# Fewer, longer steps for the mixers beside the projections of a hybrid decoder layer

## The chip, the cores and the metric

The kernel runs on one core of a Trainium2 chip. The metric is device time in microseconds (us) of one execution. The engines are named as the profile names them: PE is the matrix engine TensorE (PEld its weight loads), DVE is VectorE, ACT is ScalarE, POOL is GpSimd, SP is SyncE, which here issues the DMAs. A product on PE reads its operands from on-chip memory and writes to one of eight accumulation banks (PSUM), from which ACT or DVE must take the result before the bank can be used again; taking it out is called evacuation.

## The reference

One inference step of a one-layer decoder trunk, for a prompt of 2048 tokens and 8 samples of 8 tokens (64 columns), model width 1024, all in float32:

- h = RMSNorm(x) * (1 + scale) + shift, with scale and shift from a conditioning vector.
- One input projection h @ w_in. Its columns go to two mixers.
  - A gated DeltaNet (4 heads, 128 x 128 state): a causal convolution of width 4 and SiLU on q, k, v; q and k normalised; then chunks of tokens, in each of which a triangular system (A + I) is solved, giving T, and a state S of each head is carried from chunk to chunk: u = T(v b) - T(k b e^G) S, o = (q e^G) S + (q k^T decay) u, S = S c + k_tail^T u. The output is normalised and gated by SiLU(z).
  - Sliding-window attention (8 query heads, 2 key and value heads of 64, window 128) with a relative-position bias and a learned sink in each softmax.
- x = x + gate * (mixers' outputs @ w_out), then RMSNorm, a gated feed-forward block with a causal convolution of width 3 between up- and down-projection, a residual, and a last RMSNorm.

Outputs are the tokens of prompt and samples and the new states and caches.

## The kernel before

Tokens lie along the free dimension, channels along the 128 partitions. The prompt is worked in two halves: the first of two blocks of 512 tokens, the second of blocks of 384, 384 and 320 (the last 64 of these are the samples). Each float32 projection is done as three products of a high and a low part: w_hi*h_hi, w_hi*h_lo and w_lo*h_hi. `gemm_steps` (L360) does these three for one 128-deep slice and then yields; this is one projection step. `project` (L398) runs over weight tiles and blocks and calls an evacuation behind each block.

The mixers are written as Python generators that yield between their stages. They work on chunks of 128 tokens, 8 a half:

- `front` (L675): loads k, q and v of a chunk from DRAM (tiles kq and xv), transposes k and q (kq_ps), takes squares on ACT, computes decays (d_ps, Dc), transposes v (v_ps), makes the matrices A and M (am_ps, tile AM), writes A to DRAM and reads its 16 x 16 diagonal blocks back (G), inverts these in 14 steps of DVE (TU, L764 and L766), writes the inverses to DRAM (tu_d) and reads them back as T and U.
- `levels` (L806): joins the 16 x 16 inverses to 32, 64 and 128 by pairs of products z_ps and u_ps, each with an evacuation between (Y).
- `scan` (L878): p_ps, o_ps, uu_ps, s_ps, o_ps: the chunk's part of the recurrence; `gated_norm` follows, with a transpose ot_ps and a DMA to the tensor mixd.
- `attend` (L970): splits keys and queries into high and low parts on ACT, transposes v (vt_ps), scores for four groups of heads (as_ps), softmax, transposes (pt_ps), masks on POOL (PT), products with v (pv_ps).

`mixers` (L2029) goes over the chunks of a half. For chunk c it runs scan(c), attend(c), levels(c+1) and front(c+2) in `lockstep` (L384): one round takes each generator to its next yield. `ahead` (L2023) does the front of the first two chunks. `beside` (L374) runs rounds of a mixer and, between them, a share of projection steps, which the list SHARE gives: 5.5 steps a round for the first half's mixers, beside the in-projection of the second half, and 4.0 for the second half's, beside the up-projection of the first. What a mixer does not use up is done behind it.

This sets the order in which the program is written. A planner in the framework then orders each engine's instructions: it plays the program through with modelled durations and gives an engine the instruction of the earliest place in the program (its priority) that is ready by that model. On the chip, each engine then takes its instructions in the planned order and waits by semaphore for operands. `tc.issue_after(x)` keeps the block's instructions on x's engine behind x in that order.

The accumulation banks: 2 for the projections ("acc"), 2 for front ("fr"), 2 for attention ("at"), 1 each for scan ("sc") and for levels and gates ("st"). `gates` (L449) computes decays and betas for a half from a small projection (ba_ps), transposed in pieces of 128 tokens (bat_ps) and reduced on DVE.

Of the kernel before, what the change touches and what calls it, by code (L numbers as in the profile page):

```python
# [30 lines left out]
H = 4  # L31
# [63 lines left out]
def kernel(  # L95
# [264 lines left out]
    def gemm_steps(ps, w, hb, n, ks=range(KT), first=None, last=None):  # L360

        (wh, wl), (hh, hl) = w, hb
        for k in ks:
            for i, (a, b) in enumerate(((wh, hh), (wh, hl), (wl, hh))):
                nc.tensor.matmul(ps[:, :n], a[:, k, :], b[:, k, :n],  # L365
                                 start=first is not False and k == ks[0] and i == 0,
                                 stop=last is not False and k == ks[-1] and i == 2)
            yield True
# [6 lines left out]
    def beside(steps, filler, share):  # L375

        due = 0.0
        for _ in steps:
# [70 lines left out]
    def gates(hf, h, wb, pool):  # L449
# [8 lines left out]
        for bi, c0, n, np_ in blocks(hf):  # L458
# [9 lines left out]
            for t in range(0, n, P):  # L468
# [4 lines left out]
                j += 1  # L473
# [201 lines left out]
    def front(c, d, pool, rows=P):  # L675
        c0 = P * c
        smp = rows < P
        two = 1 if smp else 2
        tle = cst[:rows, C_SLE:C_SLE + rows] if smp else cst[:, C_TLE:C_TLE + P]
        tgt = tgtr[:rows, P:] if smp else tgtr[:, :P]  # L680
# [7 lines left out]
        for i in range(2):  # L688
            nc.gpsimd.tensor_tensor(gm[i][:rows], over_h(tle, rows), over_i(ghl[:rows, i, c].bitcast(F32), rows),
                                    ALU.mult)  # L690
        ss = pool.tile([P, H, 2], F32, tag="ss", name="ss")
        kq_ps = []
        for i in range(2):
# [7 lines left out]
            yield True  # L701
# [23 lines left out]
        v_ps = bank("v_ps", "fr")  # L725
        for h in range(H):
            nc.tensor.transpose(v_ps[:rows, P * h:P * h + P], xv[:, h, :], ident)
        vb = pool.tile([P, H, P], F32, tag="vb", name="vb", bufs=two)
        nc.vector.tensor_tensor(vb[:rows], heads(v_ps)[:rows], over_i(nr[:rows, :, 0], P), ALU.mult)
        yield True  # L730

        AM = pool.tile([P, H, 2, rows], F32, tag="AM", name="AM", bufs=1 if smp else 2)
        for s in range(2):
# [7 lines left out]
            yield True  # L741
# [18 lines left out]
        for j in range(1, BS - 1):  # L760
# [6 lines left out]
            if j % 5 == 0:  # L767
                yield True
# [24 lines left out]
        d.update(vb=vb, Kt=Kt, kq=kq, MT=MT, nr=nr)  # L793
# [12 lines left out]
    def levels(d, pool):  # L806
# [58 lines left out]
        yield True  # L865
# [58 lines left out]
    def gated_norm(c, d, o, xz, pool, rows=P):  # L924
# [12 lines left out]
        for _ in range(4):  # L937
            yield True
# [6 lines left out]
        yield True  # L945
# [23 lines left out]

    def attend(c, c1, ac, kt, loaded, pool):  # L970
# [3 lines left out]
        qs, sv, new = loaded.pop()  # L974
        for b in new:
# [1229 lines left out]
```

## Time and profile before

| what | value |
|---|---|
| time, median of 3 runs | 2621.32 us (2616.15 to 2625.87) |
| the profiled execution, its own time | 2624.72 us |
| its span from first to last instruction | 2622.9 us |
| granted clock of TensorE | 0.996 |
| stage with the first half's mixers (about 345 to 750 us) | 405 us, PE busy 395.5 |
| stage with the second half's front and mixers (about 930 to 1378 us) | 448 us, PE busy 445.1 |
| sample mixers and the rest of their up-projection (to about 1530 us) | 152 us, PE busy 150.1 |

Busy time is the time in which at least one instruction of an engine ran. Matmuls are pipelined: two that follow one another overlap in the profile, so the distance between their starts tells more than their lengths. In a row of instructions, "x8" means eight in a row of one kind, and "[0.28 <-DMA T<-tu_d]" that the engine was idle for 0.28 us until that transfer came. One matmul of plain float32 operands shows as two instructions.

### The profile page before, as it was taken

How to read it: one execution, taken by the hardware profiler on the slowest of the kernel's cores; microseconds unless marked ns; L12 is line 12 of the kernel's file. 1: busy time of each engine (PE TensorE's matmuls, PEld its weight loads, DVE VectorE, ACT ScalarE, POOL GpSimd, SP SyncE). 2: the span in 40 equal slices, each digit the busy share in tenths (PEclk: the TensorE clock that was granted, in tenths of full speed). 3: DMA queues.
4: the chain of work that ended last, by engine and by line, in shares of the span. 5: the costliest groups of instructions: out<-in, count | busy, mean ns of one | idle time of the engine just before them, and what ended most of it. 6: DMA issues, size and time to landing. Idle time of an engine off the chain costs nothing.

```text
span 2622.9 us, 45390 instructions
## 1 busy us (share of the span) xinstructions
PE 2553.1 (97%) x16424; PEld 2216.3 (84%) x16424; DVE 1840.1 (70%) x3633; ACT 1288.9 (49%) x3140; POOL 795.7 (30%) x708
## 2 busy tenths in 40 slices
PE   6999999999999999999999999999999999999998
PEld 5677888888888787777877789999999997888998
DVE  6475579896544687788768665886777675687676
ACT  5464365554343455555544353654555554454453
POOL 2064143334232322233121123345565520022022
PEclk9999999999999999999999999999999999999999
DMA  7787554343556353333345266325555447676454
GB/s 274 252 296 270 155 144 120 98 121 83 125 187 204 116 136 90 106 103 90 85 141 203 95 209 222 116 73 166 169 168 180 167 162 273 210 243 201 144 192 135
DMA packets 315820, 427.62 MB, mean 163 GB/s; under 512 B 82211, under 2 KB 206212, under 8 KB 315332
## 3 DMA queue, kind: packets, MB, share of 16 engines
q1 hardware_dynamic: 315596, 424.73, 50.9%
q8 instruction: 129, 2.11, 0.3%
q14 instruction: 95, 0.78, 0.1%
HBM read 305.07 MB, written 120.57 MB: 162 GB/s over the span
## 4 chain that ended last, share of the span: by engine, by line
PE 74%; DVE 10%; DMA 7%; ACT 3%; issue 2%; POOL 2%; SPq 1%; POOLq 0%; DVEq 0%; ACTq 0%
PE up_ps L365 17%; PE dn_ps L1825 16%; PE in_ps L365 12%; PE op_ps L365 5%; PE uq_b L1611 5%; PE uq_c L1611 2%; PE uq_u L1611 2%; PE uq_g L1611 2%; PE pv_ps L1033 1%; DVE ev L573 1%; PE uq_a L1611 1%; DMA mt<-mixd 1%; PE as_ps L996 1%; PE u_ps L811 1%; DVE w_lo L357 1%
## 5 line engine op out<-in xcount | busy, mean ns | idle before, releaser
L365 PE MATMUL in_ps<-hi,w_hi 128*128 128x512 f32 (+2 forms) x880 | 318.1, 364 | 4.7 <-DVE ev L629 2.1
L365 PE MATMUL in_ps<-lo,w_hi 128*128 128x512 f32 (+2 forms) x880 | 314.7, 358 | 1.5 <-DVE lo L297 1.1
L365 PE MATMUL up_ps<-hi,w_hi 128*128 128x512 f32 (+2 forms) x808 | 314.3, 389 | 1.5 <-ACT sg L568 1.5
L365 PE MATMUL up_ps<-lo,w_hi 128*128 128x512 f32 (+2 forms) x808 | 313.5, 388 | 1.9 <-DVE lo L297 1.9
L365 PE MATMUL in_ps<-hi,w_lo 128*128 128x512 f32 (+2 forms) x880 | 314.7, 358 | 0.0
L365 PE MATMUL up_ps<-hi,w_lo 128*128 128x512 f32 (+2 forms) x808 | 311.6, 386 | 0.1
L1825 PE MATMUL dn_ps<-th,wh 128*128 128x512 f32 (+2 forms) x796 | 271.4, 343 | 5.1 <-ACT th L1713 5.1
L1825 PE MATMUL dn_ps<-tl,wh 128*128 128x512 f32 (+2 forms) x796 | 272.6, 343 | 0.0
L1825 PE MATMUL dn_ps<-th,wl 128*128 128x512 f32 (+2 forms) x796 | 271.1, 342 | 0.0
L357 DVE TENSOR_TENSOR w_lo<-w_raw,w_hi 128x1024 fp32r<-128x1024 f32 x115 | 145.2, 1263 | 87.4 <-ACT w_hi L356 82.5
L356 ACT CAST w_hi<-w_raw 128x1024 fp32r<-128x1024 f32 x126 | 132.0, 1048 | 139.6 <-PE op_ps L365 52.5
L365 PEld LDWEIGHTS in_ps<-hi,w_hi 128*128 128x128 f32 x880 | 165.4, 189 | 30.8 <-issue 8.6
L365 PEld LDWEIGHTS in_ps<-lo,w_hi 128*128 128x128 f32 x880 | 166.0, 189 | 21.2 <-issue 3.8
L365 PEld LDWEIGHTS up_ps<-lo,w_hi 128*128 128x128 f32 x808 | 152.3, 188 | 37.4 <-issue 10.7
L365 PEld LDWEIGHTS up_ps<-hi,w_hi 128*128 128x128 f32 x808 | 152.3, 188 | 35.9 <-issue 8.6
L365 PEld LDWEIGHTS in_ps<-hi,w_lo 128*128 128x128 f32 x880 | 165.8, 188 | 17.8 <-issue 3.6
L365 PEld LDWEIGHTS up_ps<-hi,w_lo 128*128 128x128 f32 x808 | 152.1, 188 | 31.5 <-issue 5.3
L1713 ACT CAST wh<-wr 128x512 fp32r<-128x512 f32 x149 | 92.2, 619 | 165.2 <-PE dn_ps L1825 110.0
L1825 PEld LDWEIGHTS dn_ps<-th,wh 128*128 128x128 f32 x796 | 150.9, 190 | 21.1 <-ACT th L1713 5.5
L573 DVE SCALAR_TENSOR_TENSOR ev<-rb,cw,ev 128x512 f32<-128x512 f32 (+2 forms) x180 | 140.3, 785 | 38.6 <-ACT ev L566 36.9
L1825 PEld LDWEIGHTS dn_ps<-tl,wh 128*128 128x128 f32 x796 | 151.0, 190 | 16.1 <-DVE tl L1714 0.4
L1825 PEld LDWEIGHTS dn_ps<-th,wl 128*128 128x128 f32 x796 | 151.1, 190 | 15.4
(565 smaller groups left out, 6514.3 us busy)
## 6 DMA issues: line engine op xcount, KB each, us to landing
w_raw<-in_w_upT_dram SPq DMA_DIRECT2D x50, 512.0 KB
wada<-in_w_ada_dram SPq DMA_DIRECT2D x48, 512.0 KB
w_raw<-in_w_inT_dram SPq DMA_DIRECT2D x44, 512.0 KB
wr<-ws_d SPq DMA_DIRECT2D x88, 256.0 KB
w_raw<-in_w_outT_dram SPq DMA_DIRECT2D x34, 512.0 KB
d<-act_d SPq DMA_DIRECT2D x33, 512.0 KB
wr<-in_w_downT_dram SPq DMA_DIRECT2D x66, 256.0 KB
proj<-ev SPq DMA_DIRECT2D x44, 256.0 KB
```

What stands on the lines that cost most here:

```text
L356: nc.scalar.copy(hi, raw)
L357: (eng or nc.vector).tensor_tensor(lo, raw, hi.bitcast(F32), ALU.subtract)
L365: nc.tensor.matmul(ps[:, :n], a[:, k, :], b[:, k, :n], start=first is not False and k == ks[0] and i == 0, stop=last is not False and k == ...
L573: nc.vector.scalar_tensor_tensor(out, src(j), w[:, j:j + 1], out, ALU.mult, ALU.add)
L811: mm = lambda out, a, b, r, c: nc.tensor.matmul(out, a, b, start=True, stop=True, tile_position=(r, c))
L996: nc.tensor.matmul(banks[v][:, 256 * g:256 * g + 256 - P * k0], qs[:, 2 * (g0 + g) + v], t[:, v, :2 - k0].rearrange("p w j -> p (w j)"), s ...
L1033: nc.tensor.matmul(pv_ps[64 * v:64 * v + 64, :], (vprev[0], vt)[half][:, 64 * v:64 * v + 64], PT[v, half], start=half == k0, stop=half == 1)
L1611: nc.tensor.matmul(bk[t][:, :nb], u[:, k], v[:, k], start=new and k == 0 and y == 0, stop=k == KG - 1 and y == 2, skip_group_check=True)
L1713: nc.scalar.copy(h, raw)
L1825: nc.tensor.matmul(acc[m, s][:, :n], w[q, i][a][:, c], th[b][:, v], start=new and i == 0 and y == 0, stop=i == KH - 1 and y == 2, skip_gro ...
```

## The change

Five edits. (1) Yields are taken out and moved, so that a chunk's generators have 6 yields or fewer: 7 rounds a chunk instead of 11. `front` does both transposes and squares in one round and both am_ps in one; the transpose of v moves behind the fifth step of the inversion; `attend` transposes v behind the scores, masks both halves in one round, and splits the next chunk's keys and queries at its own end (`attend_split`). (2) The loads of `front` become `front_load`, called for chunk c+3 in chunk c, behind four rounds. (3) SHARE rises to 8.0, 8.4 and 6.1; the sample stage keeps 4.0 by an entry of its own. (4) With `behind`, a round's instructions on PE are ordered behind the last product of `gemm_steps` that was written before it, and everything in the round gets a priority 60 places earlier. This holds for both halves' mixers and the second half's `ahead`. (5) `gates` transposes all pieces of a block into one bank and reduces them together.

```diff
@@ gemm_steps
-                nc.tensor.matmul(ps[:, :n], a[:, k, :], b[:, k, :n],
+                mm = nc.tensor.matmul(ps[:, :n], a[:, k, :], b[:, k, :n],
...
+            product[:] = [mm.ins]
             yield True
+    product = []
-    def beside(steps, filler, share):
+    def beside(steps, filler, share, behind=False):
         due = 0.0
-        for _ in steps:
+        while True:
+            with (tc.issue_after(product[0]) if behind and product else nullcontext()), (tc.high_priority(OFFSET) if behind else nullcontext()):
+                if not next(steps, None):
+                    break
             due += share
@@ gates
-                nc.tensor.transpose(ps[:rows, t:t + 32], ev[:32, t:t + rows], cst[:32, C_ID:C_ID + 32])
-                nc.vector.tensor_reduce(ba[:rows, j, :], ps[:rows, t:t + 32].rearrange("p (a r) -> p r a", r=16)[:, 0:8],
-                                        mybir.AxisListType.X, ALU.add)
+                nc.tensor.transpose(ps[:rows, 32 * i:32 * i + 32], ev[:32, t:t + rows], cst[:32, C_ID:C_ID + 32])
+            for i, m, rows in ((0, n // P, P), (n // P, 1, n % P)):
+                if rows:
+                    v = ps[:rows, 32 * i:32 * i + 32 * m].rearrange("p (j a r) -> p j r a", a=2, r=16)[:, :, 0:8]
+                    nc.vector.tensor_reduce(ba[:rows, j:j + m, :], v, mybir.AxisListType.X, ALU.add)
+                    j += m
@@ front
-    def front(c, d, pool, rows=P):
+    def front_load(c, d, pool, rows=P):
...
+        d.update(kq=kq, xv=xv, gm=gm)
+        yield True
+
+    def front(c, d, pool, rows=P):
...
+        kq, xv, gm = d["kq"], d["xv"], d["gm"]
...
                 nc.scalar.activation(jk[:rows], ps[:rows, h, :], AF.Square, accum_out=ss[:rows, h, i:i + 1])
-            yield True
...
-        v_ps = bank("v_ps", "fr")
-        for h in range(H):
-            nc.tensor.transpose(v_ps[:rows, P * h:P * h + P], xv[:, h, :], ident)
-        vb = pool.tile([P, H, P], F32, tag="vb", name="vb", bufs=two)
-        nc.vector.tensor_tensor(vb[:rows], heads(v_ps)[:rows], over_i(nr[:rows, :, 0], P), ALU.mult)
-        yield True
...
                                                ALU.mult)
-            yield True
...
-            if j % 5 == 0:
+            if j == 5:
+                yield True
+                v_ps = bank("v_ps", "fr")
+                for h in range(H):
+                    nc.tensor.transpose(v_ps[:rows, P * h:P * h + P], xv[:, h, :], ident)
+                vb = pool.tile([P, H, P], F32, tag="vb", name="vb", bufs=two)
+                nc.vector.tensor_tensor(vb[:rows], heads(v_ps)[:rows], over_i(nr[:rows, :, 0], P), ALU.mult)
+            elif j == 10:
                 yield True
...
                 nc.sync.dma_start(dst, TU[nb * h:nb * h + nb, x])
+        yield True
@@ levels
         nc.vector.tensor_copy(U[low, :, high], ut[low, 0])
-        yield True
@@ gated_norm
-        for _ in range(4):
-            yield True
+        yield True
+        yield True
...
-        yield True
@@ attend
+    def attend_split(kt, loaded):
+        qs, _, new = loaded[0]
+        for b in new:
+            for t in kt:
+                nc.scalar.copy(t[:, :, b % 2], t[:, :, b % 2].bitcast(F32))
+        nc.scalar.copy(qs, qs.bitcast(F32))
...
-        qs, sv, new = loaded.pop()
-        for b in new:
-            for t in kt:
-                nc.scalar.copy(t[:, :, b % 2], t[:, :, b % 2].bitcast(F32))
-        nc.scalar.copy(qs, qs.bitcast(F32))
-        vt_ps = bank("vt_ps", "at")
-        nc.tensor.transpose(vt_ps[:, :P], sv, ident)
...
-        yield True
+        qs, sv, _ = loaded.pop()
...
             yield True
+        vt_ps = bank("vt_ps", "at")
+        nc.tensor.transpose(vt_ps[:, :P], sv, ident)
...
                 nc.gpsimd.tensor_tensor(PT[v, half], pt, tri[half], ALU.mult)
-            yield True
+        yield True
+        if loaded:
+            attend_split(kt, loaded)
+        yield True
         pv_ps = bank("pv_ps", "at")
...
-        yield True
         vprev[0] = vt
@@ the plan
-    SHARE = (5.4, 5.5, 4.0, 2.05, (2.0, 1.4), 5.0, (1.3, 2.0), 8.0)
+    SHARE = (8.0, 8.4, 6.1, 2.05, (2.0, 1.4), 5.0, (1.3, 2.0), 8.0, 4.0)
+    OFFSET = 60
@@ ahead
-            yield from front(c0, ds[c0], pool)
-            yield from lockstep(levels(ds[c0], pool), front(c0 + 1, ds[c0 + 1], pool))
+            yield from front_load(c0, ds[c0], pool)
+            yield from lockstep(front(c0, ds[c0], pool), load_next(c0 + 1, pool))
+            yield from lockstep(levels(ds[c0], pool), front(c0 + 1, ds[c0 + 1], pool), load_next(c0 + 2, pool))
+
+        def load_next(c, pool):
+            for _ in range(4):
+                yield True
+            yield from front_load(c, chunks[c], pool)
@@ mixers
+            attend_split(kt, loaded)
...
+                if c + 3 < c1:
+                    g.append(load_next(c + 3, pool))
@@ the calls
-            beside(mixers(0, mp), filler, SHARE[1])
+            beside(mixers(0, mp), filler, SHARE[1], True)
...
-            beside(ahead(1, mp), filler, SHARE[2])
-            beside(mixers(1, mp), filler, SHARE[2])
+            beside(ahead(1, mp), filler, SHARE[2], True)
+            beside(mixers(1, mp), filler, SHARE[2], True)
...
-            beside(lockstep(sample_delta(sp), sample_attend(sp), weight_sums(range(6, KH), sp, nc.vector)), filler, SHARE[2])
+            beside(lockstep(sample_delta(sp), sample_attend(sp), weight_sums(range(6, KH), sp, nc.vector)), filler, SHARE[8])
```

More of the change, by code (lines that the diff above doesn't have):

```diff
@@ L6 @@
-from contextlib import ExitStack
+from contextlib import ExitStack, nullcontext
 import numpy as np
@@ L364, in gemm_steps @@
             for i, (a, b) in enumerate(((wh, hh), (wh, hl), (wl, hh))):
-                nc.tensor.matmul(ps[:, :n], a[:, k, :], b[:, k, :n],
-                                 start=first is not False and k == ks[0] and i == 0,
-                                 stop=last is not False and k == ks[-1] and i == 2)
+                mm = nc.tensor.matmul(ps[:, :n], a[:, k, :], b[:, k, :n],
+                                      start=first is not False and k == ks[0] and i == 0,
+                                      stop=last is not False and k == ks[-1] and i == 2)
+            product[:] = [mm.ins]
             yield True
@@ L467, in gates @@
             ps = st_bank("bat_ps")
-            for t in range(0, n, P):
+            for i, t in enumerate(range(0, n, P)):
                 rows = min(P, n - t)
-                nc.tensor.transpose(ps[:rows, t:t + 32], ev[:32, t:t + rows], cst[:32, C_ID:C_ID + 32])
-                nc.vector.tensor_reduce(ba[:rows, j, :], ps[:rows, t:t + 32].rearrange("p (a r) -> p r a", r=16)[:, 0:8],
-                                        mybir.AxisListType.X, ALU.add)
-                j += 1
+                nc.tensor.transpose(ps[:rows, 32 * i:32 * i + 32], ev[:32, t:t + rows], cst[:32, C_ID:C_ID + 32])
[4 more added lines that the diff above has]
+                    j += m
             yield True
@@ L670, in attn_consts @@
         return NB, own, sink, nsink
-    def front(c, d, pool, rows=P):
+    def front_load(c, d, pool, rows=P):
         c0 = P * c
         smp = rows < P
-        two = 1 if smp else 2
         tle = cst[:rows, C_SLE:C_SLE + rows] if smp else cst[:, C_TLE:C_TLE + P]
-        tgt = tgtr[:rows, P:] if smp else tgtr[:, :P]
         kq = pool.tile([P, H, 2, rows], F32, tag="kq", name="kq", bufs=1 if smp else 3)
@@ L690, in front @@
                                     ALU.mult)
+        d.update(kq=kq, xv=xv, gm=gm)
+        yield True
+    def front(c, d, pool, rows=P):
+        smp = rows < P
+        two = 1 if smp else 2
+        tle = cst[:rows, C_SLE:C_SLE + rows] if smp else cst[:, C_TLE:C_TLE + P]
+        tgt = tgtr[:rows, P:] if smp else tgtr[:, :P]
+        kq, xv, gm = d["kq"], d["xv"], d["gm"]
         ss = pool.tile([P, H, 2], F32, tag="ss", name="ss")
@@ L1011, in attend @@
             yield True
+        vt_ps = bank("vt_ps", "at")
+        nc.tensor.transpose(vt_ps[:, :P], sv, ident)
+        vt = keep.tile([P, P], F32, tag="vt", name="vt", bufs=2)
+        nc.scalar.copy(vt, vt_ps[:, :P])
+        if c == NCH - 1:
+            nc.sync.dma_start(O["p_swa_v"], vt)
         if c + 1 < c1:
@@ L1054, in sample_delta @@
         nc.sync.dma_start(S0, I["state_ssm"].rearrange("p (b h) d -> p b h d", b=NB_S))
+        yield from front_load(NCH, d, sp, LS)
         yield from front(NCH, d, sp, LS)
```

6 lines of the change are left out of this document (1 added, 5 removed).

## The prediction

> **What bounds the kernel now.** I read the page first, then busy time by stage, then the waits of TensorE in the two mixer stages, then TensorE's timeline over one chunk of each.
>
> ```profile
> span 2622.9 us, 45390 instructions
> ...
> PE 2553.1 (97%) x16424; PEld 2216.3 (84%) x16424; DVE 1840.1 (70%) x3633; ACT 1288.9 (49%) x3140; POOL 795.7 (30%) x708
> ...
> PEclk9999999999999999999999999999999999999999
> ```
>
> TensorE (PE) is the bound, at full clock. Busy time by stage says the same of the stages that the change touches (columns: stretch, length, busy time of PE, PEld, DVE, ACT, POOL, then clock and DMA):
>
> ```profile
> 345.00:750.00 405.00, 395.48 (x3243) 350.97 (x3243) 305.73 (x892) 210.59 (x702) 137.56 (x131) 1.00 0.41 111
> 930.00:1378.00 448.00, 445.14 (x3199) 349.40 (x3198) 356.59 (x924) 229.88 (x709) 110.13 (x96) 1.00 0.38 104
> 1378.00:1530.00 152.00, 150.05 (x741) 111.48 (x740) 106.58 (x197) 62.61 (x158) 21.51 (x11) 1.00 0.45 156
> ```
>
> 345 to 750 holds the first half's mixers beside in-projection, 930 to 1378 the second half's beside up-projection. PE is busy for 98% and 99% of them, VectorE (DVE) for 75% and 80%, ScalarE (ACT) for about half. So a gain cannot come from idle time of PE as the page counts it; it has to be time in which PE is "busy" and moves no columns. The timeline shows that time where the products of a mixer stand between two projection products (start us, length, engine, line, tiles):
>
> ```profile
> 507.48 0.34 PE L365 MATMUL in_ps<-hi,w_lo 128*128 128x384 f32 x1
> 507.75 0.68 PE L811 MATMUL z_ps<-T,AM 64*64 64x64 f32 x8
> 508.35 0.45 PE L365 MATMUL in_ps<-hi,w_hi 128*128 128x384 f32 x1
> 508.64 0.34 PE L365 MATMUL in_ps<-lo,w_hi 128*128 128x384 f32 x1
> 508.81 0.33 PE L365 MATMUL in_ps<-hi,w_lo 128*128 128x384 f32 x1
> ...
> 523.91 0.33 PE L365 MATMUL in_ps<-hi,w_lo 128*128 128x384 f32 x1
> 524.09 0.62 PE L716 MATMUL d_ps<-gm,tgtr 128*128 128x512 f32 x2
> 524.54 0.34 PE L365 MATMUL in_ps<-hi,w_hi 128*128 128x384 f32 x1
> 524.72 0.34 PE L365 MATMUL in_ps<-lo,w_hi 128*128 128x384 f32 x1
> ...
> 528.67 0.34 PE L365 MATMUL in_ps<-hi,w_lo 128*128 128x384 f32 x1
> 528.85 0.60 PE L727 MATMUL v_ps<-cst,xv 128*128 128x128 f32 x4
> 529.21 0.42 PE L365 MATMUL in_ps<-hi,w_hi 128*128 128x384 f32 x1
> 529.47 0.34 PE L365 MATMUL in_ps<-lo,w_hi 128*128 128x384 f32 x1
> ```
>
> Two projection products start 0.17 us apart (508.64, 508.81). At z_ps the one before lasts 0.27 to the next start (0.10 over) and the one behind 0.29 (0.12 over): this interruption costs **0.22 us** beside its own work. At v_ps it is 0.01 + 0.09 = **0.10 us**, at d_ps 0.01 + 0.01 = **0.02 us**. The mean of the three is 0.11 us; I call it the edge.
>
> How many such groups a chunk has, I counted on the same view, a group being all mixer products between two projection products: from the p_ps product of one chunk to that of the next there are 19 in the first half, and over the 53 us that follow 1091 there are 16 in the second. The first and the last of each:
>
> ```profile
> 500.25 1.05 PE L884 MATMUL p_ps<-S,kq 128*128 128x128 f32 x8
> ...
> 556.39 0.34 PE L811 MATMUL u_ps<-inv,Y 32*32 32x32 f32 x10 [0.20 <-ACT Y L841]
> ...
> 558.93 1.05 PE L884 MATMUL p_ps<-S,kq 128*128 128x128 f32 x8
> ...
> 1091.23 0.67 PE L811 MATMUL u_ps<-inv,Y 64*64 64x64 f32 x8
> ...
> 1138.81 1.93 PE L1033 MATMUL pv_ps<-PT,vt 128*64 128x512 f32 x6
> ```
>
> The second thing PE loses is waits for operands. The longest of each mixer stage (engine, line, waited for: us in total, times, longest):
>
> ```profile
> PE u_ps L811 <- DVE Y L859: 2.7, 1, 2.7
> PE pv_ps L1033 <- POOL PT L1028: 1.8, 3, 1.0
> PE u_ps L811 <- ACT Y L841: 1.5, 3, 0.7
> ...
> PE p_ps L884 <- DVE xz L942: 1.2, 2, 0.8
> PE z_ps L811 <- DMA T<-tu_d: 1.0, 3, 0.5
> PE u_ps L811 <- DVE Y L859: 0.5, 1, 0.5
> ```
>
> These six make 8.7 us in 13 waits, 0.67 us each. They are small because ready projection products nearly always cover a mixer's latency.
>
> **The change part by part.** *Steps.* A chunk's longest generator falls from 11 rounds to 7, and the share of projection steps per round rises from 5.5 to 8.4 (first half) and from 4.0 to 6.1 (second): 60.5 against 58.8 and 44 against 42.7 a chunk. So projection work beside a chunk stays the same and no mixer product is added or removed; only its place changes. A round grows from 405 / 8 / 11 = 4.6 us to 405 / 8 / 7 = 7.2 us. If all products of a round stand together, a chunk has 7 groups. Some will not: a round's second product can be late (v_ps now follows DVE work within its chain, vt_ps follows the last scores), and the gates keep their own ba_ps and bat_ps places. I allow 2 strays, 9 groups. Removed: (19 - 9) x 8 + (16 - 9) x 8 = 136 groups, x 0.11 = **15 us**. Bounds: 7 groups and 0.22 us each give (12 + 9) x 8 x 0.22 = 37 us; at the 0.02 us of d_ps, or if the strays are as many as now, nothing.
>
> *Behind and 60 places up.* The order edge holds a round's products behind the preceding round's last projection product, which takes away early strays; the priority makes the same products, and all of the mixers' DVE, ACT, POOL and queue work, go ahead of the projection work that comes within 60 places. This is the edit that can add waits. ACT in the first half, by shape:
>
> ```profile
> L700 ACT ACTIVATE junk<-kq_ps 128x128 bf16<-128x128 f32 x48 | 13.3, 277 | 1.2 <-PE kq_ps L697 0.3
> L590 ACT ACTIVATE rb<-ev 128x384 f32<-128x384 f32 x24 | 12.6, 527 | 26.7 <-DVE ev L573 26.7
> ...
> L563 ACT COPY rb<-in_ps 128x384 f32<-128x384 f32 x24 | 11.3, 472 | 3.6 <-PE in_ps L365 3.4
> ...
> L700 ACT ACTIVATION_READ_ACCUMULATOR junk<-kq_ps 128x1 f32 x48 | 9.5, 199 | 0.0
> ```
>
> The front's first round now has both squarings: 8 x (277 + 199) ns = 3.8 us on ACT in one piece, where it had 1.9 us twice. Behind it stand the projection's evacuations (L563, 0.47 us, and its companion). An accumulation bank has 24 products x 0.17 = 4.1 us until PE wants it back, plus the mixer products in between; 3.8 us fits under that, so I cost it at nothing; without that cover it is the rest of 3.8 us once a chunk. The d_ps product, one round later, wants one of the two banks that the squarings read: 7.2 us later, against 3.8 us of ACT work.
>
> *Waits.* Longer rounds put 7.2 us instead of 4.6 between a product and the one that needs its evacuation. That serves the level products (2.7, 1.5, 0.5), pv_ps (now two rounds behind PT) and z_ps behind T (1.0); p_ps behind xz is not helped. I take 6 of the 8.7 us, bounds 0 and 8.7. For new waits I put 3 of 0.67 us, **+2 us**, bounds 0 and half of the 2 x 8 x 7 = 112 rounds, 37 us.
>
> *Loads ahead.* front_load issues three DMAs on SP and two products on POOL one chunk earlier:
>
> ```profile
> L689 POOL TENSOR_TENSOR gm<-cst,ghl 128x512 fp32r<-128x512 f32 x10 | 12.0, 1203 | 5.4 <-PE d_ps L716 4.5 <-DVE AM L738 1.0
> ```
>
> and SP's own waits in the same stage:
>
> ```profile
> SPq L635 <- DVE ev L591: 39.6, 11, 10.2
> ```
>
> The same number of both; POOL is busy for 34% of the stage and its 2 x 1.2 us lie beside other work. On SP they pass stores of the projection that hold the queue (L635, 39.6 us over 11 waits); a load comes in the fifth of seven rounds, three rounds or some 20 us ahead of its front, and a store delayed by three issues holds an ev buffer, not PE. Cost 0. The keys' split on ACT moves from the head of a chunk to its sixth round, work unchanged. In the second half the attention's bias loads share the kq buffers, all three of which are now taken when mixers start; they wait for the first chunk's o_ps, two rounds, with projection products as cover: 0 on PE.
>
> *Gates.* The transposes of a block now fill one bank one behind the other, and 4 reductions replace 9 in the second half's gates (2 replace 8 in the first); their groups are in the 19. *Sample.* Its share stays 4.0 on fewer rounds, so more up-projection is left behind it, all of it PE work in any order: 0.
>
> Sum: -15 - 6 + 2 = **-19 us**. The profiled execution took 2624.72 us (span 2622.9 and 1.8 around it), so 2605.7; the median shown is 3.4 us under that execution, so **2602 us** against 2621.32.
>
> **The rivals.** *Edges are free (2615 us).* If most groups are like d_ps, grouping is worth nothing and only the 6 us of waits go. For it: d_ps at 0.02 us. Against: z_ps at 0.22 and v_ps at 0.10, both seen. [...]
>
> *The planner places them as before (2621 us).* The order edge binds a round's products only to what lies before; nothing holds the next projection products behind them. If operands come late in the plan, groups stay scattered. For it: a product that late data splits today, with another mixer product put in between,
>
> ```profile
> 1106.37 0.23 PE L811 MATMUL z_ps<-T,AM 32*32 32x16 f32 x2 [0.28 <-DMA T<-tu_d]
> ...
> 1106.98 0.71 PE L871 MATMUL uu_ps<-vb,inv 128*128 128x128 f32 x4
> 1107.62 0.23 PE L811 MATMUL z_ps<-T,AM 32*32 32x16 f32 x2
> ```
>
> Against: rounds of 7.2 us, in which such data has more time to come.
>
> *Everything merges at the dear price (2578 us).* 37 us of edges and 6 of waits off. For it: the price at z_ps, and six such level products a chunk. Against: v_ps and d_ps.
>
> *Waits multiply (2644 us, slower).* Grouped products are issued in order on PE; one whose operand is late holds its whole group and the projection behind it, where it now stands alone at a place where it was ready. Place: d_ps behind the squarings, u_ps behind Y. With the 0.67 us of a wait, 31 of the 112 rounds eat the 21 us of gain; at every second round it is 56 x 0.67 - 15 = 23 us slower. For it: ACT stands 26.7 us in all behind one kind of instruction (L590), which waits for DVE, so late evacuations do queue. Against: PE waited 13 times for long in 16 chunks, and rounds get longer. [...]
>
> **How the numbers follow.** About 0.5%, 13 us, can be told from no change. Forecast (2592 to 2611): 0.47, of which 0.41 is faster by more than that and 0.06 within. Everything merges: 0.15, faster. Edges free: 0.16, and placed as before: 0.10, both within. Waits multiply: 0.12, slower. Faster 0.56, same 0.32, slower 0.12. The range 2580 to 2632 holds all but the lower part of the merging case and the larger part of the last one.
>
> **What would show it.** Right: about 9 groups a chunk in PE's timeline; chunks of about 56.5 and 51 us instead of 58.7 and 53; the six waits down to some 3 us; the stages behind 1530 us unmoved. Wrong: chunks of the old length with half the groups (edges were free), or rows of PE waiting on DVE or ACT that sum to 20 us and more (waits multiply), or 15 and more groups a chunk (not placed).

## The result and the profile after

The changed kernel takes 2643.99 us (median of six runs, 2638.55 to 2647.82). The kernel before, run beside it, takes 2625.93 us (median of six, 2616.15 to 2628.45). The ratio is **1.0072, 95% interval 1.0059 to 1.0085**: 18 us slower. The forecast was 2602 us, 19 us faster than the 2621 it started from and 24 us faster than the kernel before in these runs; its range ended at 2632. The profiled execution of the changed kernel took 2638.55 us, and 2624.72 us is that of before.

Where the time came from shows first in when the stages begin. Three marks, each the first product of its kind in TensorE's timeline: the output projection of the first half starts at 779.5 us before and 781.5 after (2 us later); the first quarter of the last up-projection at 1730.9 and 1745.1 (14.2 later); the down-projection at 2152.7 and 2166.2 (13.5 later). So the stage with the first half's mixers gave and took the same, and the one with the second half's lost some 12 us. Page and busy time by stage of the changed kernel, the same two stretches as before:

```profile
span 2636.8 us, 45371 instructions
...
PE 2556.4 (97%) x16424; PEld 2223.9 (84%) x16424; DVE 1837.0 (70%) x3622; ACT 1287.6 (49%) x3141; POOL 798.0 (30%) x708
...
345.00:750.00 405.00, 393.14 (x3259) 354.34 (x3258) 315.61 (x891) 210.13 (x704) 140.74 (x132) 1.00 0.41 113
930.00:1378.00 448.00, 440.28 (x3134) 344.85 (x3133) 344.89 (x911) 223.16 (x691) 102.09 (x88) 0.99 0.36 96
```

In the first stretch PE starts 3259 products where it started 3243; in the second 3134 where it started 3199, with 5 us more idle time and a clock of 0.99. Its waits there (engine, line, waited for: us in total, times, longest), first half from 345 to 760 us, then second half from 900 to 1410 us:

```profile
PE ot_ps L958 <- POOL o L953: 2.4, 2, 1.3
PE z_ps L829 <- ACT cout L578: 1.9, 2, 1.4
PE in_ps L365 <- ACT sb L588: 1.7, 2, 1.2
PE in_ps L365 <- ACT ev L575: 1.5, 1, 1.5
...
PE ot_ps L958 <- POOL o L953: 1.7, 1, 1.7
PE z_ps L829 <- DVE T L869: 1.6, 2, 1.3
PE o_ps L908 <- DVE vb L903: 1.2, 2, 0.8
```

None of these seven was among the six quoted of before; two kinds of them, z_ps behind T and o_ps behind vb, did stand in the first half of before, with 1.1 us each. The old ones did shrink (pv_ps behind PT is gone, u_ps behind Y fell from 4.7 us in all to 2.1), and others took their place: ot_ps, now two rounds behind the scaling of o instead of four, and projection products behind evacuations on ACT.

And the products stand otherwise than the change was to place them. TensorE's timeline of the changed kernel, second half (start us, length, engine, line, tiles; the pair behind the names is the size of the piece of the array that the product uses):

```profile
1114.98 0.60 PE L888 MATMUL uu_ps<-vb,inv 128*128 128x128 f32 x4
1115.52 0.23 PE L829 MATMUL z_ps<-T,AM 32*32 32x16 f32 x2
1115.67 0.49 PE L888 MATMUL uu_ps<-vb,inv 128*128 128x128 f32 x2
1116.09 0.23 PE L829 MATMUL z_ps<-T,AM 32*32 32x16 f32 x2
1116.25 0.49 PE L888 MATMUL uu_ps<-vb,inv 128*128 128x128 f32 x2
...
1121.12 0.49 PE L916 MATMUL s_ps<-u,Kt 128*128 128x128 f32 x2
1121.54 0.21 PE L829 MATMUL u_ps<-inv,Y 32*16 32x16 f32 x2
1121.68 0.49 PE L916 MATMUL s_ps<-u,Kt 128*128 128x128 f32 x2
1122.10 0.21 PE L829 MATMUL u_ps<-inv,Y 32*16 32x16 f32 x2
1122.24 0.49 PE L916 MATMUL s_ps<-u,Kt 128*128 128x128 f32 x2
```

The rows above the dots lie within one "group" by the prediction's count, the rows below within another: no projection product stands between the rows of either. Inside, two kinds alternate two by two. From one pair of s_ps to the next is 0.56 us; where products of these forms follow their like, the median distance of starts is 0.11 us for s_ps and 0.007 for u_ps, so two and two would take 0.24. One turn there and back costs 0.32 us.

**An account of TensorE.** To put the three losses side by side I took, for each product, the time from its start to the next start, less the median distance of that kind to its like in the kernel before. What is left went to one of three: half-clock stretches (the granted clock in the record is 0.5); a wait, where the record has an operand arriving more than 0.12 us after the product could have started; and the rest, called changes, which is mostly what changing from one kind to another costs. First half: from 247.8 us to the first output-projection product; second half: from the first up-projection product to the first of the quarters.

| kernel | first half: length, changes, waits, half clock | second half: length, changes, waits, half clock |
|---|---|---|
| before | 531.7, 33.9, 15.9, 1.5 | 859.2, 47.5, 14.9, 1.4 |
| after | 533.7, 29.7, 20.3, 3.1 | 871.5, 53.5, 17.4, 4.7 |
| e1 few steps alone | 535.4, 29.3, 20.0, 4.5 | 861.1, 37.4, 20.1, 8.1 |
| e2 second half plain | 531.9, 29.5, 19.8, 1.5 | 859.2, 38.4, 19.2, 6.1 |
| e6 old steps, edge and priority | 545.3, 40.4, 19.3, 2.9 | 860.2, 43.7, 18.1, 3.4 |
| e7 eight rounds | 532.9, 29.7, 18.6, 3.1 | 862.4, 50.8, 12.5, 3.3 |
| e10 lead 30 | 536.5, 29.5, 20.2, 6.0 | 854.0, 45.5, 8.9, 4.2 |
| e12 lead 30, second half plain | 533.1, 30.0, 20.6, 1.5 | 842.1, 35.0, 10.2, 1.5 |
| e13 before with lead 30 | 534.5, 33.5, 16.3, 3.6 | 855.9, 47.7, 9.2, 3.2 |

The products' own time is the same within 3 us in every row (480 to 483 and 795 to 796). One profiled execution differs from the next of the same kernel: in e8, whose first part is the kernel before, the first half took 541.0 us, not 531.7. 4.3 us of that lie ahead of the mixers: 247.8 us is the start in every row, and the first kq_ps product runs at 247.8 us before, 247.9 after, 251.4 in e6 and 252.1 in e8. So the account says which kind of loss moved; how much a kernel gains or loses is said by the timed runs.

Against before, the changed kernel has 4.2 us less of changes in the first half, which 4.4 us of waits and 1.6 us of half clock eat up; and 6.0 us more of changes, 2.5 us more of waits and 3.3 us more of half clock in the second. The line between changes and waits is not sharp: where every idle gap over 0.12 us counts as a wait, whatever ended it, the second half has 4.2 us more of changes and 4.9 us more of waits.

### The profile page after: what moved, and what is told of

Read it like the earlier page. It is cut to its first block, busy times and chain, and to the rows that moved or that the text cites. A ratio compares the mean times of both kernels' runs of the same rounds, so it can differ in the third digit from the quotient of the medians.

```text
span 2636.8 us, 45371 instructions
## 1 busy us (share of the span) xinstructions
PE 2556.4 (97%) x16424; PEld 2223.9 (84%) x16424; DVE 1837.0 (70%) x3622; ACT 1287.6 (49%) x3141; POOL 798.0 (30%) x708
## 3 DMA queue, kind: packets, MB, share of 16 engines
q1 hardware_dynamic: 315596, 424.73, 50.7%
## 4 chain that ended last, share of the span: by engine, by line
PE 57%; DVE 7%; DMA 5%; issue 2%; POOL 2%; ACT 2%; SPq 1%; POOLq 0%; DVEq 0%; ACTq 0%
PE up_ps L365 17%; PE dn_ps L1846 16%; PE op_ps L365 6%; PE uq_b L1632 4%; PE in_ps L365 2%; PE uq_c L1632 2%; PE uq_u L1632 2%; PE uq_g L1632 2%; DMA rawu<-in_w_upT_dram 1%; PE uq_a L1632 1%; DVE TU L776 1%; DVE gt L774 1%; DMA rawg<-in_w_upT_dram 1%; PE pv_ps L1054 1%; DVE w_lo L357 1%
## 5 line engine op out<-in xcount | busy, mean ns | idle before, releaser
L365 PEld LDWEIGHTS in_ps<-lo,w_hi 128*128 128x128 f32 x880 | 166.4, 189 | 19.2 <-DVE lo L297 2.5
L1846 PEld LDWEIGHTS dn_ps<-tl,wh 128*128 128x128 f32 x796 | 151.0, 190 | 16.3 <-DVE tl L1735 0.7
```

The lines of the kernel that those rows point to most:

```text
L365: mm = nc.tensor.matmul(ps[:, :n], a[:, k, :], b[:, k, :n], start=first is not False and k == ks[0] and i == 0, stop=last is not False and ...
L1846: nc.tensor.matmul(acc[m, s][:, :n], w[q, i][a][:, c], th[b][:, v], start=new and i == 0 and y == 0, stop=i == KH - 1 and y == 2, skip_gro ...
```

## Experiments

The kernel before ran beside each; all timed ones in five rounds. Two theories stood at the start. A: the 60 places of priority cost, most in the second half. B: the longer steps cost (squarings in one piece, ot_ps two rounds after its scaling).

**e1: the steps alone.** Neither order edge nor priority anywhere.

```diff
-            beside(mixers(0, mp), filler, SHARE[1], True)
+            beside(mixers(0, mp), filler, SHARE[1])
...
-            beside(ahead(1, mp), filler, SHARE[2], True)
-            beside(mixers(1, mp), filler, SHARE[2], True)
+            beside(ahead(1, mp), filler, SHARE[2])
+            beside(mixers(1, mp), filler, SHARE[2])
```

> The steps as changed (fewer and longer, loads a chunk ahead, gates in one bank), but neither the order edge nor the 60 places, in either half. Theory A, the 60 places cost, most in the second half, where they put products among the projection that are not ready: without them both halves lose that, so 2644 less the 14.6 us of the second half and some of the first half's, 2615 to 2630 us, with PE's waits in 900 to 1410 us back near the 4 us of the kernel before. Theory B, the longer steps cost (both squarings in one piece, the output transposed two rounds after its scaling instead of four): 2638 to 2646 us, the waits on o and on ACT's evacuations stay.

2627.26 us, ratio to before 1.0003 (0.9992 to 1.0013). The loss is gone, as A said; but the waits of the second half did not go back to 4 us as A expected. They grew, on the transfer of T above all:

```profile
PE z_ps L829 <- DMA T<-tu_d: 3.6, 7, 1.8
PE uu_ps L888 <- DVE o L910: 1.8, 1, 1.8
PE z_ps L829 <- DVE T L869: 1.6, 1, 1.6
```

So the fewer, longer steps by themselves do save changes (10 us in the second half by the account) and give all of it back to waits (5 us) and half clock (7 us).

**e2: edge and priority in the first half alone.** The second pair of lines of e1's diff.

> The changed kernel with the order edge and the 60 places in the first half alone. Theory A: the second half's stretch returns to within 5 us of the kernel before, 2626 to 2633 us. Theory B: nothing of the second half's 14.6 us comes back, 2640 to 2646 us.

2623.92 us, 0.9998 (0.9988 to 1.0009): all of the 18 us comes back with the second half alone, a little more than theory A expected. Theory A holds, B falls. The stretch of the changed kernel's timeline shown above has its counterpart here:

```profile
1101.88 1.05 PE L888 MATMUL uu_ps<-vb,inv 128*128 128x128 f32 x8
1103.19 0.60 PE L829 MATMUL z_ps<-T,AM 32*32 32x16 f32 x6
...
1108.53 0.38 PE L829 MATMUL u_ps<-inv,Y 32*16 32x16 f32 x32
1108.74 0.47 PE L829 MATMUL u_ps<-Y,inv 32*32 32x16 f32 x24
1109.14 0.94 PE L916 MATMUL s_ps<-u,Kt 128*128 128x128 f32 x6
```

uu_ps stands whole, and u_ps runs through 56 in a row between two pieces of s_ps. Over the second half s_ps and u_ps change places 2 + 1 times here and 24 + 22 times in the changed kernel, uu_ps and z_ps once against 27 times, z_ps and projection 29 against 48 times.

**e3: the order edge without the priority.**

```diff
-            with (tc.issue_after(product[0]) if behind and product else nullcontext()), (tc.high_priority(OFFSET) if behind else nullcontext()):
+            with (tc.issue_after(product[0]) if behind and product else nullcontext()):
```

> The changed kernel with the order edge and without the 60 places. If it is the 60 places that cost (theory A): as the kernel with neither, within 4 us, 2615 to 2630 us. If the order edge costs, by holding products that are ready behind a projection product: 2640 us and more.

2629.7 us, 1.0010 (0.9996 to 1.0023): within 0.3% of both e1 and before. The edge is not what costs.

**e4: the priority without the order edge.** The other half of that line is kept.

> The changed kernel with the 60 places and without the order edge. In the planned order of TensorE this makes 334 groups of mixer products in the first half and 196 in the second, against 91 and 124 with the edge, 315 more, the products being the same. If a group costs the 0.11 us of the prediction: 35 us more, 2679 us. If edges are free (0.02 us): 2650 us. At the 0.22 us of z_ps: 2713 us.

2674.93 us, 1.0183 (1.0165 to 1.0202): near the middle expectation, but not for its reason alone. By the account the first half has 24 us more of changes than the changed kernel (389 groups in the timeline against 115, 0.09 us for each one more) and another 24 us of half clock. The timeline shows both. Mixer products stand one pair at a time between projection products:

```profile
368.86 0.44 PE L365 MATMUL in_ps<-hi,w_hi 128*128 128x384 f32 x1
369.24 0.21 PE L829 MATMUL u_ps<-inv,Y 32*16 32x16 f32 x2
369.38 0.44 PE L365 MATMUL in_ps<-lo,w_hi 128*128 128x384 f32 x1
...
374.64 0.69 PE L365 MATMUL in_ps<-hi,w_hi 128*128 128x384 f32 x1
375.26 0.29 PE L829 MATMUL u_ps<-Y,inv 32*32 32x16 f32 x2
375.47 0.69 PE L365 MATMUL in_ps<-lo,w_hi 128*128 128x384 f32 x1
```

A projection product and two u_ps take 0.52 us (368.86 to 369.38), where projection products alone start 0.17 apart: again 0.33 us for one turn there and back. Then the clock falls, and the same takes 0.83 us. Busy time in stretches of 3.4 us around that moment (stretch, length, PE, PEld, DVE, ACT, POOL, clock):

```profile
367.96:371.38 3.42, 3.42 (x21) 1.92 (x21) 2.69 (x11) 2.54 (x6) 2.68 (x2) 1.00 0.23 64
371.38:374.80 3.42, 3.42 (x15) 1.92 (x13) 3.13 (x10) 3.42 (x16) 2.10 (x2) 0.50 0.27 81
374.80:378.20 3.40, 3.40 (x13) 1.93 (x13) 3.40 (x9) 2.53 (x10) 2.60 (x3) 0.50 0.00 0
```

PE counts as busy without a break, and its clock is halved all the same, for 17 us.

**e5: a lead of 60 steps.** In the changed kernel the second half's first kq_ps product runs at 919.3 us, 45.7 us behind the first up-projection product (873.6), though its place in the program is the very front: before, it is 918.8, 47.1 behind. By then 57 projection steps have run that were written beside later rounds. The row of the changed kernel:

```profile
919.32 0.93 PE L715 MATMUL kq_ps<-cst,kq 128*128 128x128 f32 x7
```

The kernel of this run lets 60 of them run first by the program too:

```diff
             inverse_tiles(mp)
+            for _ in range(60):
+                next(filler)
             beside(ahead(1, mp), filler, SHARE[2], True)
```

> The changed kernel, with 60 projection steps (some 35 us of up-projection) run off ahead of the second half's first mixer work. In the changed kernel that work's first products run 45 us behind the place where the program has them, because the memory of their tiles comes free late. Theory C, the 60 places cost in the second half because its mixers lag their place in the program, so that the priority pulls products that are never ready together: with the lag gone the second half groups as the first does, and the time is that of the kernel with the 60 places in the first half alone or better, 2612 to 2628 us. Theory D, the 60 places cost wherever the projection beside the mixers is the up-projection: 2638 to 2646 us.

2624.34 us, 0.9994 (0.9985 to 1.0004). Theory C holds as to the loss: with the lead the priority costs nothing against e2. The hoped-for gain did not come: in this profile the output projection behind waits 8.3 us for split weights (op_ps behind DVE w_lo, 2.7 us in e2). The 60 steps are missing there as cover: with the same lead these waits are 9.3 us in e9, with 30 steps 3.4 us in e10 and 1.8 us in e12.

**e6: order edge and priority on the old steps.** The kernel before with the lines of `beside` and the two calls changed.

> The kernel before, steps, loads and gates unchanged, with the order edge and the 60 places added in both halves. If the 60 places cost by themselves in the second half: 2635 to 2645 us. If they cost only with the longer steps, whose groups are larger: within 5 us of the kernel before, 2621 to 2631 us.

2638.02 us, 1.0042 (1.0026 to 1.0059): they cost 11 us by themselves. In this profile the loss lies in the first half, not the second, so the expectation named the right sum and the wrong place. The second half's mixers lag there as in the changed kernel (48.7 us), and the stage took 1 us more than before: what was lost in the changed kernel's second half takes the other edits as well as the priority.

**e7: eight rounds a chunk.** e2 with one more yield before ot_ps, one more at the head of `levels`, shares of 7.35 and 5.34.

> The kernel with the order edge and the 60 places in the first half alone, with eight rounds a chunk instead of seven: one more round between the scaling of o and its transposes, one more between the loads of T and the first z_ps product; shares 7.35 and 5.34. If the gain of the fewer groups is eaten by waits, and by the half-clock stretches that follow them: waits of PE on POOL o and on the DMA of T go from some 8 us over both halves to under 3 us, half-clock stretches become fewer, and the time is 2610 to 2619 us. If the waits go and the time stays at 2622 to 2628 us, the waits were not what ate it.

2627.79 us, 1.0009 (1.0000 to 1.0019). The waits on o are gone, that on T's transfer is down to 1.1 us; in the second half all waits went from 19.2 to 12.5 us and half clock from 6.1 to 3.3. The time did not follow, because changes rose from 38.4 to 50.8 us: with another round the products stand in 167 groups up to the second output projection, where the kernel before has 159 and e2 142. Waits and changes are traded for each other here.

**e8: the two prices by themselves.** The kernel before, with products on constants added behind its end; what they compute is thrown away. Left out below: behind each 48 products a transpose, one to four copies of its result on VectorE, and a transpose that reads the last copy.

```diff
+        for rep in range(16):
+            stream("s_together", 24)
+            for kind in ("bz", "bv", "bd"):
+                small(kind)
+        for rep in range(16):
+            for kind in ("bz", "bv", "bd"):
+                stream("s_apart", 8)
+                small(kind)
+        for width in (128, 640, 1152, 1664):
+            for rep in range(16):
+                stream(f"s_gap{width}", 48)
...
```

> The kernel before with a series of products added behind its end, on constants, in fixed order on TensorE (its results are not stored). First 16 times 24 projection-like products (128x384) and then 8 products of 64x64, 4 transposes and 2 products of 128x512 as one group; then 16 times the same products as three groups, each behind 8 of the 24. The difference of the two, per two groups added, is the price of a group beside its own work: 0.2 us a repetition by the prediction's 0.11 us, 0.04 us if edges are free. Then four series of 16 times 48 products and one wait of TensorE for a chain on VectorE, of one to four instructions (an estimate from VectorE's rows: some 0.6, 1.2, 1.8 and 2.4 us). If a short wait costs half-clock stretches besides itself, the granted clock falls below 1 in the series with the longer waits and not in those with the shorter ones, and a repetition is up to 1.7 us longer than its products and its wait; if only long idle time does that, the clock stays at 1 in all four.

This is one profiled execution. Together, a repetition takes 6.30 us, apart 6.38: **0.04 us for each group more**, not 0.11. The timeline says why. First the three kinds in one group, then each alone:

```profile
2662.04 1.14 PE L2138 MATMUL bz<-sm 64*64 64x64 f32 x16
2663.11 0.66 PE L2142 MATMUL bv<-cst,sm 128*128 128x128 f32 x4
2663.52 0.71 PE L2145 MATMUL bd<-mv,wt 128*128 128x512 f32 x2
...
2760.45 1.14 PE L2138 MATMUL bz<-sm 64*64 64x64 f32 x16
2761.52 1.66 PE L2132 MATMUL s_apart<-mv,wt 128*128 128x384 f32 x8
2763.03 0.60 PE L2142 MATMUL bv<-cst,sm 128*128 128x128 f32 x4
2763.38 1.66 PE L2132 MATMUL s_apart<-mv,wt 128*128 128x384 f32 x8
```

bz takes 1.07 us to the next start in both, whether a transpose or a projection-like product follows. What costs is going between the 128*128 array and a 64*64 piece of it, and both series do that once a repetition. Where bz stands alone, the stream's last product ahead of it takes 0.27 us to the next start instead of 0.17, the first bz 0.11 instead of 0.06, the last 0.15 instead of 0.06, and the stream's first product behind it 0.28 instead of 0.17: 0.34 us for one turn there and back, near the 0.32 of s_ps and u_ps. Between the 128*128 kinds almost nothing is lost: the last transpose of bv takes 0.08 us less to the next start than the others, and the stream's product behind it 0.09 us more.

The second part, waits of rising length. The rows of the wait in the third and fourth series, and busy time and clock over each of the four series:

```profile
3299.87 0.30 PE L2166 MATMUL gb<-cst,g 128*128 128x128 f32 x1 [1.67 <-DVE g L2162]
...
3310.90 0.30 PE L2166 MATMUL gb<-cst,g 128*128 128x128 f32 x1 [2.27 <-DVE g L2162]
```

```profile
2829.00:2975.00 146.00, 140.25 (x801) 135.67 (x799) 4.37 (x15) 0.00 (x0) 0.00 (x0) 1.00 0.00 1
2976.00:3133.00 157.00, 139.84 (x800) 135.51 (x799) 14.22 (x32) 0.00 (x0) 0.00 (x0) 1.00 0.00 1
3134.00:3299.00 165.00, 139.14 (x795) 134.74 (x794) 23.07 (x47) 0.00 (x0) 0.00 (x0) 1.00 0.00 1
3300.00:3484.00 184.00, 149.44 (x800) 145.07 (x799) 31.77 (x61) 0.00 (x0) 0.00 (x0) 0.94 0.00 1
```

Waits of 1.67 us leave the clock at 1; waits of 2.27 us bring six half-clock stretches of 3.41 us in sixteen repetitions, and a repetition with one takes 12.6 us instead of 11.03. So a wait of 2.27 us can cost 1.6 us on top of itself.

**e9 to e14: what the longer steps are worth where the mixers stand at their place.**

e9 is e5 with the second half plain.

> The changed kernel with the 60 steps of up-projection run off first, and the order edge and the 60 places in the first half alone. With the lag gone, does the priority gain anything in the second half? If it groups products usefully there: this is slower than the kernel with lead and priority (2624 us), by 3 us and more. If the priority is harmless but useless: 2622 to 2627 us, the same.

2627.19 us, 1.0002 (0.9992 to 1.0012): the priority neither gains nor costs there.

e10 is e5 with 30 steps instead of 60.

> The changed kernel, order edge and 60 places in both halves, with 30 steps (some 18 us) run off first instead of 60. The lag is 45 us, so half of it stays. If the cost of the priority goes with the lag: between 2624 and 2644 us, 2628 to 2638 us. If any lead is enough for the memory of the tiles to come free: 2618 to 2625 us, since 30 steps more are left as cover for the output projection's weights, which the 60 steps took away.

2619.05 us, 0.9971 (0.9959 to 0.9982), the second of the two: faster than both kernels. The first kq_ps product still runs 48 us behind the first up-projection product, so the 30 steps fell into time in which the mixers could not have begun.

e11 is the kernel before with 60 steps of lead.

> The kernel before with the 60 steps run off first, nothing else changed. If the lag costs the kernel before nothing (its products have no priority): 2622 to 2630 us, the same within 4 us. If the lead alone is a gain, as the 12 us of its second mixer stage in the changed kernel could mean: under 2620 us.

2635.09 us, 1.0039 (1.0025 to 1.0054): slower, against both expectations. Its output projection waits 4.4 us for a split of mixer outputs and 4.3 us for weights.

e12 is e10 with the second half plain (no edge, no priority).

> The kernel with the 30 steps of lead, and the order edge and the 60 places in the first half alone: beside the kernel with the same lead and both in both halves (2619 us) it tells whether the priority gains anything once its mixers stand at their place. If grouping by priority has a worth of its own in the second half: 2622 to 2628 us. If the longer steps and the lead make the gain and the priority nothing: 2617 to 2621 us.

**2611.16 us, 0.9942 (0.9929 to 0.9956)**: 14 us faster than the kernel before and the fastest of all. Neither expectation went that far: the priority costs 8 us in the second half even with the lead. All of PE's waits from 900 to 1410 us, and its busy time in the stretch from 930 us:

```profile
PE ot_ps L958 <- POOL o L953: 0.7, 1, 0.7
PE up_ps L365 <- ACT sg L577: 0.3, 1, 0.3
```

```profile
930.00:1378.00 448.00, 447.26 (x3279) 360.95 (x3279) 344.42 (x942) 238.81 (x740) 108.70 (x98) 1.00 0.40 111
```

3279 products start in the 448 us that held 3199 before and 3134 in the changed kernel, at full clock.

e13 is the kernel before with 30 steps of lead, e14 is e12 with no edge and no priority in the first half either.

> The kernel before with 30 steps of up-projection run off ahead of its second mixer stage, steps unchanged. If the 14 us of the kernel with fewer, longer steps and the same lead come from the lead: 2609 to 2616 us. If the longer steps bring them, and the lead only lets them (the waits that longer steps bring go when the mixers stand at their place): 2620 to 2632 us.

> Fewer, longer steps and the lead of 30, with neither order edge nor 60 places in either half. Beside the same kernel with both in the first half (2611 us): if they gain something there, 2614 to 2622 us; if they cost there as in the second half, 2600 to 2607 us; if nothing, within 3 us of 2611.

e13: 2623.08 us, 0.9987 (0.9976 to 0.9998). e14: 2613.24 us, 0.9949 (0.9934 to 0.9965). So the lead alone is worth some 3 us, the longer steps with the lead another 10 to 12, and edge and priority in the first half nothing that can be told apart (2611 against 2613 us).

## Why the prediction was wrong

**What bounds the kernel: right.** TensorE still does, and time moved only where its starts moved.

**The edge, "0.11 us" for every group: wrong in kind.** The 0.02 us at d_ps was read rightly. The 0.22 us at z_ps was too little, because it left out the mixer products' own rows: eight z_ps that start 0.06 us apart need 0.47 us, and the row quoted shows 0.60 to the next start, so the interruption costs 0.35 us, as the turn in e8 does. The 0.10 us at v_ps was no loss: four transposes that start 0.11 us apart need 0.44 us, the row shows 0.36, and the 0.09 us by which the product behind lasts longer makes up for it. So the price was 0.35 us once and 0.02 or less twice. That the mean of these comes out near 0.11 as well is luck; taking a mean over them was the mistake. In these rows and in e8 the price does not hang on standing between projection products but on going from the whole array to a piece of it and back, and the prediction's rows showed the piece: 64*64 at z_ps (0.35 us), 128*128 at the other two (0.02 or less). Putting a z_ps product into a group saves little (0.04 us for each group in e8, so the rival "edges are free" was nearer) where its neighbour there uses the whole array, as bv does in e8. Between two small pieces no such price shows in e2's rows above: the 32 u_ps on 32*16 take 0.21 us up to the first on 32*32, and 32 starts 0.007 us apart need 0.22. Where the change did save time on changes, 10 us in e1's second half, half of it was another thing: the pv_ps products (128*64) stay together more (left for a projection product 10 times instead of 19; from their starts to the next starts they take 18.1 us in all instead of 23.5).

**Nine groups a chunk: wrong.** Counted from p_ps to p_ps, the first half has 14 on average (15, 14, 15, 15, 15, 8) where it had 18, the second 14 to 19 behind its first chunk, where it had 11 to 17. "15 and more: not placed" was the sign set for this, and the second half shows it. The rival of that name put the cost at nothing; it is not nothing, because a group can be as broken inside as outside.

**"Behind and 60 places up" at +2 us: the step that failed.** e2 against the changed kernel gives it: about 19 us in the second half (0.9998 against 1.0072). That is about half of the 37 us between a gain of 19 and a loss of 18; the other half lies in the first two terms, -15 and -6, which e1 puts at +1 us together (1.0003). In the two profiles that half is 12.3 us longer: 15.1 us more of changes (53.5 against 38.4), 1.8 us less of waits, 1.4 us less of half clock. In the timeline it is s_ps against u_ps and uu_ps against z_ps, changing places 73 times (4 times in e2), and z_ps cut by projection products; at half of the 0.32 us turn, 69 changes more make 11 of the 15 us. The cost follows this count where the lead changes: with 30 steps the priority brings 42 such changes against 10 and costs 8 us (e10 against e12), with 60 steps 7 against 5 and costs nothing (e5 against e9). I had asked what the priority does to DVE, ACT and the queues, and not what it does between two mixer generators of the same round. That the lag of the second half's mixers makes this worse is shown by the leads (18 us over before without, 7 us under with 30 steps); how the planner comes from the lag to this order is not shown.

**Waits, -6 and +2: wrong in sign.** The old waits went as forecast, but new ones came: in all, 4.4 us more in the first half and 2.5 us more in the second. Rounds became fewer as well as longer: two of 7.2 us behind POOL's o are less than four of 4.6, and T's transfer now stands in the last of seven rounds, two before the z_ps that reads it. With the lead these waits go (14.9 to 9.2 us in e13, 19.2 to 10.2 in e12), which speaks for projection work beside the mixers that had been used up before its time; that it was this and not the later start alone is argued, not shown.

**Costs at nothing.** The squarings in one piece: hidden, as far as the runs show, but for in_ps and z_ps waiting on ACT's evacuations (5.1 us in three rows above) and once 1.9 us of d_ps behind the squares in e7; the share of this that is due to the squarings was not taken apart. Loads ahead and bias loads: no wait in any row. The gates were not tried alone. What the sum left out altogether is the clock: the half rate costs 1.6 and 3.3 us more than before, and 7 us more in e1's second half.

**The rival that ended near the time, "waits multiply" (2644 us), had another mechanism.** It asked for 20 us of waits. There are 7 us more of them; by the account the rest is 1.8 us more of changes and 4.9 us more of half clock, both halves together. That a late product holds those behind it on PE, as this rival had it, shows in e8: s_gap works on constants and starts 0.06 us behind gb (3310.90, then 3310.96), not in the 2.27 us for which gb waits. The time fits by chance.

**Chunks of 56.5 and 51 us as a sign: a poor one.** The first half's chunks did get shorter, 50.7 us on average (404.5 to 708.4 us, six of them) after 53.1 (392.8 to 711.2); the stage did not, for the chunks began 12 us later and projection products run to its end. The second half's got longer, 51.4 us on average (1043.2 to 1351.5, six of them) after 46.7 (1044.0 to 1324.3): the 53 us of the prediction was one chunk, longer than the others, so the 51 of the sign was met by a stage that had become slower.

**What was right in the end:** fewer, longer steps are worth about 0.4% here, 10 to 12 us, not far from the 15 us of the sum's first term, but only without the priority in the second half and with 30 projection steps run ahead, neither of which the change had. As the price of 0.11 us was wrong in kind, the nearness of the two sizes is luck.

## What to carry to other kernels

Read in TensorE's rows which piece of the array a product uses before pricing an interruption: between projection products a turn from the whole array into a piece of it and back cost 0.23 us (before, 56 u_ps in a row) and 0.35 us (before, eight z_ps on 64*64) here, and 0.32 us between mixer products, and a change between whole-array products 0.02 us or less (d_ps and v_ps in the prediction's rows, bv in e8). Sum the distances of starts over the whole interruption, its own products included, or such a price is misread. A priority that lifts several generators at once can make their products interleave with one another, so look inside the groups, not only at their number. And where work is interleaved by shares, check that both sides start together; 30 steps run off first turned a change that lost 18 us into one that won 7, and 14 with the priority taken out.

## What the runs showed of the hardware that was not expected

**Half a clock for a wait of 2 us.** But for the last of a run, the half-clock stretches are 3.41 us long or a multiple of it, and all begin on one grid of 3.413 us in a run: in before, those at 611.145 and 894.451 us are 283.306 us apart, 83 times 3.4133. In e8's fourth series, those six grid periods with 1.98 us of idle time and more were followed by one, those with 1.83 us and less were not. There, 1.98 us of idle time within a period were enough. The sixteen profiles bear this out between 260 and 1740 us: every grid period there with more than 1.89 us of idle time is followed by half a clock (before: 2.84 and 2.22 us are, 1.89 is not). But some with less are too, 1.47 us in the changed kernel and down to 0.82 us in e10, so idle time is not the whole cause.

**Half a clock without any wait.** In e4 the clock stays at 0.50 for 17 us while PE is busy for all of it (17.00 us of 371 to 388, mean clock 0.51), at first during single projection products that change with pairs of small ones. So busy time in the profile is not what the clock goes by there. What it does go by the runs do not settle.
